# Two plain pairs of feature tiles in the first FFN, rms made before the token sums, squares summed on DVE, unit loads issued six units ahead

## The chip, the cores and the metric

The kernel runs on one core of a Trainium2 chip. Its engines work side by side, each through its own list of instructions, and wait for one another by semaphores: PE (TensorE: matmuls; PEld is its loading of weights), DVE (VectorE), ACT (ScalarE), POOL (GpSimd) and SP (SyncE, which issues DMAs only). The metric is the device time of one launch in microseconds (us), the median over runs; lower is better.

## The reference, cut to what matters

One layer of a streaming encoder on 512 tokens of width 1024, in fp32. The change touches the two FFNs and the sums of squares ahead of them; the mixer between them stays.

```python
def rms_norm(x, w):
    return x * lax.rsqrt(jnp.mean(x * x, axis=-1, keepdims=True) + EPS) * w

def swiglu(h, w_gate, w_up, w_down):
    return (jax.nn.silu(h @ w_gate) * (h @ w_up)) @ w_down

# x (1, 512, 1024); w_gate, w_up (1024, 2816); w_down (2816, 1024)
x = x + 0.5 * swiglu(rms_norm(x, ffn1_norm), ffn1_w_gate, ffn1_w_up, ffn1_w_down)
x = x + hybrid_mixer(x, mix_norm, w_in, ..., w_out)      # SSD and chunked attention
x = x + 0.5 * swiglu(rms_norm(x, ffn2_norm), ffn2_w_gate, ffn2_w_up, ffn2_w_down)
return rms_norm(x, final_norm)
```

## The kernel before, in words

**Layout and precision.** x lies in SBUF as 8 blocks k of 128 model columns (partitions) by 512 tokens. An fp32 product is three matmuls on values rounded to a shorter type: hi x hi, hi x lo, lo x hi (`mm3`, L154 to L156). So every operand is split: ACT casts the high part, DVE subtracts it from the source for the low part. `usplit` does it for an FFN unit's weights of 128x1024 (L284, L286), `wsplit` for other weights (L102, L104), `split_act` for x times the norm's gain (ACT, and DVE at L162).

**An FFN.** The 22 feature tiles of 128 are 11 pairs d. A pair needs gate and up; the columns of x are halved into k 0 to 3 and k 4 to 7, which gives four weight units of 512 KB: A11 and A12 (gate, first and second half), A21 and A22 (up). Pair 0 is done plain: four units, each 8 products of `mm3` at 512 columns. Every later pair is done by a scheme of seven products P1 to P7 in place of eight half-sized ones (as in Strassen's): each of its units has the 24 matmuls at 256 columns (L479), half of the tokens. It wants sums of token halves and sums of weight units. The token sums are made by `XCombos` out of x: `weigh` (x times the gain, L384 and L386, into a buffer xw), `sum1` (L390), `sums23` (L394, L395), `sum4`, and their splits `parts1`, `parts23` (L405) and `parts4`; `parts1` is written over the second half of what `base` made (b1), which the plain units read. The weight sums are made by DMAs that POOL issues and that add onto a tile in SBUF (`more`, L323).

**rms.** The norm's factor is put in at the end, on the finished gate and up. ACT squares x, `add_squares` adds the squares up (L170, on POOL in the two openings), `rstd_begin` sums over partitions on PE (L198) and makes the root by a chain of tiny instructions on DVE (L173 to L191) and two low and high diagonals (L210), `spread` (L217) brings the factor to all partitions with two matmuls, and ACT copies it twice into rstd (L586). `plain_end` then makes h of the plain pair: L459 takes the finished gate out of its PSUM buffer, L464 the up.

**Order.** `program` lists the units: A11 A21 A12 of pair 0, P5 P1 of pair 1, A22, P6 P2 P7, then for every further pair seven units, of which P3 and P4 belong to the pair before, and the down projection's units ("D") in three blocks. `Stream.get` hands out the next unit; before it does, it splits units up to `look` ahead and issues the loads of units ahead of that, each with its own lead in units (the first number of a job's moves). Raw weights lie in four buffers `raw`; the weight sums in others. Between units the generator `early1` or `early2` runs one piece of the work on x and rms. That is the order in which the instructions are written; a scheduler then orders each engine's list by what is ready, so a list can differ from it. PSUM has three buffers mm and five aux. Loads go out on SP's queue, accumulating loads on POOL's.

**Second FFN's opening.** The output projection (`wo`, its products at L1111, the residual add into x at L1112) ends block by block; for each block the loop adds onto x, calls `base` and squares, and the second FFN's first units are split between them.

Of the kernel before, what the change touches and what calls it, by code (L numbers as in the profile page):

```python
# [12 lines left out]
ALU = mybir.AluOpType  # L13

P = 128
# [14 lines left out]
NL = 3  # L30
# [8 lines left out]
def hybrid_block(ctx: ExitStack, tc, xT, par, wgu1, wd1, win, wdt, wv, wo, rbt, wgu2, wd2, out):  # L39
# [67 lines left out]
    class Job:  # L107
# [15 lines left out]
    class Stream:  # L123


        def __init__(self):
            self.jobs, self.done, self.used, self.look = [], 0, 0, 3

        def add(self, dram, n, c):
# [145 lines left out]
    HSLOT = (22, 26, 36, 44)  # L275
# [27 lines left out]
    def ffn_weights(wgu, wd, n_last=0):  # L303
# [9 lines left out]
        def plain(key, src):  # L313
# [11 lines left out]
        for step in program(n_last):  # L325
            if step[0] == "P":
# [3 lines left out]
                if p[0] == "A":  # L330
                    n = ("A11", "A12", "A21", "A22").index(p)
                    j = Job(lambda p=p: usplit(bufs[p]), (5, None, plain(p, A[n])))
                elif p == "P1":
                    j = Job(lambda d=d: usplit(bufs["g", d]), (5, None, plain(("g", d), A[0])))
# [13 lines left out]
                jobs[p, d] = j  # L348
                ws.jobs.append(j)
# [81 lines left out]
    def ffn(xc, early, after, last=None, n_last=0):  # L431
# [13 lines left out]
        def plain(p):  # L445

            if not st:
# [797 lines left out]
```

## Time and profile before

| | |
|---|---|
| median of 3 runs | 1057.44 us (1057.33 to 1059.22) |
| the profiled execution, its span | 1058.14 us, 1056.4 us |
| granted clock of TensorE, mean of the span | 0.99 |
| PE, DVE, ACT, POOL busy | 97%, 72%, 52%, 14% |

The span is from the first to the last instruction of the profiled execution; its own time holds some 1.7 us around it. Times on the trace count from the span's start. A row of the waits says which engine (and which destination) waited for which engine's instruction: us in total, how often, the longest. A row of the timeline is a group of like instructions that follow each other: start, length, engine, line, operation, destination <- sources, shapes, count, and in brackets what the engine waited for ahead of it. A row of the stretches gives the busy time of PE, PEld, DVE, ACT and POOL, then the granted clock (1.00 is 2.4 GHz, 0.50 is 1.2 GHz), the share of the DMA engines, and GB/s.

### The profile page before, as it was taken

Reading aid. Unit: us, or ns where it says so; the run is one execution under the profiler, and the core shown is the slowest. Engines: PE = TensorE matmul, PEld = TensorE weight load, DVE = VectorE, ACT = ScalarE, POOL = GpSimd, SP = SyncE. Lnnn points to the kernel's source line nnn. Section 1 sums busy time; section 2 is a strip of 40 time slices with the busy share of each in tenths; the row PEclk is TensorE's granted clock in tenths of the full one; section 3 lists DMA queues with packets and bytes.
Section 4 is the critical chain, followed back from the end, with each engine's and each line's share of the span. In section 5 each row is a group of like instructions: output and inputs, shape, how many; then the busy total and the mean of one; then the engine's idle time right before and its main releaser. Section 6 shows DMA issues by size and latency. Waiting matters only on the chain. (4 is left out here: it accounts for less than half of the span.)

```text
span 1056.4 us, 16176 instructions
## 1 busy us (share of the span) xinstructions
PE 1026.2 (97%) x6350; PEld 915.2 (87%) x6350; DVE 757.1 (72%) x1224; ACT 547.2 (52%) x869; POOL 150.1 (14%) x163
## 2 busy tenths in 40 slices
PE   8799999999999999999999999899999999999996
PEld 6799989998899787878888788679998899989975
DVE  6987645684377778988867999797784378644754
ACT  6565424562254556656656875555552255522543
POOL 3411100110010003313201111230110011000000
PEclk9899999999999999999999999999999999999998
DMA  9878744883362422121232232926994388643612
GB/s 325 185 181 231 181 139 107 209 216 88 100 138 88 135 62 79 61 81 60 67 112 66 77 100 81 272 62 145 216 238 125 101 200 201 157 120 96 133 52 81
DMA packets 42877, 141.70 MB, mean 134 GB/s; under 512 B 4528, under 2 KB 7344, under 8 KB 42800
## 3 DMA queue, kind: packets, MB, share of 16 engines
q1 hardware_dynamic: 29040, 95.69, 27.2%
q0 software_dynamic: 11520, 41.95, 22.5%
q10 hardware_dynamic: 2240, 3.02, 0.9%
q8 instruction: 50, 0.82, 0.3%
q14 instruction: 27, 0.22, 0.1%
HBM read 138.55 MB, written 2.10 MB: 133 GB/s over the span
## 5 line engine op out<-in xcount | busy, mean ns | idle before, releaser
L479 PE MATMUL mm<-s,xw 128*128 128x256 f32 x1920 | 242.2, 284 | 0.0
L479 PEld LDWEIGHTS mm<-s,xw 128*128 128x128 f32 x1920 | 236.8, 193 | 0.2
L479 PE MATMUL aux<-s,xw 128*128 128x256 f32 x1440 | 185.7, 285 | 6.2 <-ACT xw L284 3.5
L102 ACT CAST whi<-raw 128x512 fp32r<-128x512 f32 (+1 forms) x178 | 106.0, 603 | 159.1 <-PE mm L155 121.6
L479 PEld LDWEIGHTS aux<-s,xw 128*128 128x128 f32 x1440 | 180.0, 194 | 8.0 <-ACT xw L284 3.9
L104 DVE TENSOR_TENSOR wlo<-raw,whi 128x512 fp32r<-128x512 f32 (+1 forms) x178 | 122.4, 692 | 55.6 <-ACT whi L102 55.1
L154 PE MATMUL mm<-s,whi 128*128 128x512 f32 x366 | 143.1, 392 | 4.8 <-DVE x L1112 3.1
L155 PE MATMUL mm<-s,whi 128*128 128x512 f32 x366 | 143.3, 392 | 0.0
L156 PE MATMUL mm<-s,wlo 128*128 128x512 f32 x366 | 143.2, 391 | 0.0
L284 ACT CAST xw<-raw 128x1024 fp32r<-128x1024 f32 x87 | 91.3, 1049 | 98.5 <-PE mm L479 44.1
L286 DVE TENSOR_TENSOR xw<-raw,xw 128x1024 fp32r<-128x1024 f32 x87 | 109.7, 1261 | 43.8 <-ACT xw L284 43.1
L154 PE MATMUL mm<-xw,whi 128*128 128x512 f32 x288 | 118.0, 410 | 0.0
L284 ACT CAST xw<-s 128x1024 fp32r<-128x1024 f32 x60 | 62.8, 1047 | 101.5 <-PE aux L479 61.4
L155 PE MATMUL mm<-xw,whi 128*128 128x512 f32 x288 | 113.0, 392 | 0.0
L156 PE MATMUL mm<-xw,wlo 128*128 128x512 f32 x288 | 112.9, 393 | 0.0
L323 POOL DMA_DIRECT2D s<-wgu x60 | 52.9, 905 | 402.6 <-DVE xw L286 256.9
L286 DVE TENSOR_TENSOR xw<-s,xw 128x1024 fp32r<-128x1024 f32 x60 | 73.2, 1220 | 27.0 <-ACT xw L284 27.0
L154 PEld LDWEIGHTS mm<-s,whi 128*128 128x128 f32 x366 | 69.0, 189 | 20.5 <-ACT s L384 3.5
L514 DVE TENSOR_TENSOR x<-x,mm 128x512 f32<-128x512 f32 x45 | 30.9, 687 | 74.6 <-PE mm L156 74.6
L155 PEld LDWEIGHTS mm<-s,whi 128*128 128x128 f32 x366 | 69.1, 189 | 14.4 <-DVE s L510 0.4
L156 PEld LDWEIGHTS mm<-s,wlo 128*128 128x128 f32 x366 | 69.1, 189 | 14.4
L155 PEld LDWEIGHTS mm<-xw,whi 128*128 128x128 f32 x288 | 54.3, 188 | 11.8 <-issue 1.2
(260 smaller groups left out, 1428.8 us busy)
## 6 DMA issues: line engine op xcount, KB each, us to landing
raw<-wgu SPq DMA_DIRECT2D x67, 512.0 KB, 4.4
s<-wgu POOLq DMA_DIRECT2D x60, 512.0 KB, 5.8
raw<-wd SPq DMA_DIRECT2D x32, 512.0 KB, 5.0
raw<-win SPq DMA_DIRECT2D x28, 512.0 KB, 3.5
s<-wgu SPq DMA_DIRECT2D x20, 512.0 KB, 5.6
raw<-wgu POOLq DMA_DIRECT2D x20, 512.0 KB, 6.4
raw<-wd SPq DMA_DIRECT2D x16, 384.0 KB, 3.3
raw<-wo SPq DMA_DIRECT2D x12, 512.0 KB, 3.6
```

Source lines behind the costliest of these rows:

```text
L102: S.copy(out=hi, in_=src)
L104: V.tensor_tensor(out=lo, in0=src, in1=f(hi), op=ALU.subtract)
L154: T.matmul(ps, lhsT=sh, rhs=mh, start=start, stop=False, skip_group_check=skip)
L155: T.matmul(ps, lhsT=sh, rhs=ml, start=False, stop=False, skip_group_check=skip)
L156: T.matmul(ps, lhsT=sl, rhs=mh, start=False, stop=stop, skip_group_check=skip)
L284: S.copy(out=hi, in_=src)
L286: V.tensor_tensor(out=lo, in0=src, in1=f(hi), op=ALU.subtract)
L323: return lambda: G.dma_start(out=get(), in_=src, accum_op=ALU.add)
L479: T.matmul(ps[:, j * HS:(j + 1) * HS], lhsT=sw[:, j, k], rhs=m, start=(p in ("P1", "P2", "P5") and j == 0 and k == 0 and n == 0), stop=(k ...
L514: V.tensor_tensor(out=x[:, o], in0=x[:, o], in1=ps, op=ALU.add)
```

## The change

The first FFN does two pairs plain, so pairs 0 and 1 take eight plain units in a row and the seven-product scheme begins with pair 2; the second FFN keeps one plain pair, with P1 ahead of P5. The generators are written anew: in the first FFN the squares and rms come first and the token sums behind them, `parts1` only behind A21 of pair 1, since it overwrites what that unit reads. In the second FFN rms comes with the first sums. Squares are added on DVE everywhere. The tiles of h change places (HSLOT). A plain pair 1 takes its PSUM buffers from both kinds. Loads of raw units have a lead of six units instead of five (P2 and P4 five instead of four, P5's first nine instead of ten), and a raw load is issued only when the job that holds the buffer four loads before has been split (`ws.raws`, `holds`). The diff, cut:

```diff
-            self.split, self.moves, self.parts = split, list(moves), None
+            self.split, self.moves, self.parts, self.holds = split, list(moves), None, self
...
             while self.moves and (force or ahead <= self.moves[0][0]):
                 lead, after, fn = self.moves[0]
+                if after == "raw":
+
+                    after = ws.raws[-4] if len(ws.raws) > 3 else None
+                    if not after or after.parts is not None:
+                        ws.raws.append(self.holds)
                 if after and after.parts is None:
                     assert not force
                     return
...
-                moves = [(5, None, lambda: raw.append(load(dram, n, c)))] if a == 0 else []
+                moves = [(5, "raw", lambda: raw.append(load(dram, n, c)))] if a == 0 else []
+            jobs[0].holds = jobs[-1]
...
-    def add_squares(acc, src, first, eng=None):
+    def add_squares(acc, src, first):
         if first:
             S.activation(out=acc, in_=src, func=AF.Square)
         else:
             sq = sb("fh", [P, SEQ], bufs=2)
             S.activation(out=sq, in_=src, func=AF.Square)
-            (eng or V).tensor_tensor(out=acc, in0=acc, in1=sq, op=ALU.add)
+            V.tensor_tensor(out=acc, in0=acc, in1=sq, op=ALU.add)
...
-    HSLOT = (22, 26, 36, 44)
+    HSLOT = (36, 44, 22, 26)
...
-    def program(n_last):
-
-
-        out = [("P", p, d) for p, d in (("A11", 0), ("A21", 0), ("A12", 0), ("P5", 1), ("P1", 1), ("A22", 0), ("P6", 1),
-                                        ("P2", 1), ("P7", 1))]
-        for d in range(2, ND):
+    def program(plain, n_last):
+
+
+        if plain == 1:
+            out = [("A11", 0), ("A21", 0), ("A12", 0), ("P1", 1), ("P5", 1), ("A22", 0), ("P6", 1), ("P2", 1), ("P7", 1)]
+        else:
+            out = [(a, d) for d in range(plain) for a in ("A11", "A21", "A12", "A22")]
+            out += [(p, plain) for p in ("P5", "P1", "P6", "P2", "P7")]
+        out = [("P", p, d) for p, d in out]
+        for d in range(plain + 1, ND):
             out += [("P", p, e) for p, e in (("P5", d), ("P1", d), ("P3", d - 1), ("P4", d - 1), ("P6", d), ("P2", d),
                                              ("P7", d))]
...
-                    j = Job(lambda p=p: usplit(bufs[p]), (5, None, plain(p, A[n])))
+                    j = Job(lambda k=(p, d): usplit(bufs[k]), (6, "raw", whole((p, d), A[n])))
...
                 elif p == "P2":
-                    j = Job(lambda d=d: usplit(bufs["g2", d]), (4, None, plain(("g2", d), A[1])))
+                    j = Job(lambda d=d: usplit(bufs["g2", d]), (5, "raw", whole(("g2", d), A[1])))
                 elif p == "P4":
-                    j = Job(lambda d=d: usplit(bufs["u2", d]), (4, None, plain(("u2", d), A[3])))
+                    j = Job(lambda d=d: usplit(bufs["u2", d]), (5, "raw", whole(("u2", d), A[3])))
                 elif p == "P5":
-                    j = Job(lambda d=d: usplit(view(d)), (10, jobs.get(("P3", d - 4)), first(d)),
+                    j = Job(lambda d=d: usplit(view(d)), (9, jobs.get(("P3", d - 4)), first(d)),
                             (7, None, more(sum_, A[3])))
...
+                if p == "P7":
+                    jobs["P1", d].holds = j
...
-        def plain(p):
-
-            if not st:
-                st["A1"], st["A2"] = [mmps(), mmps()], [aux(), aux()]
+        def plain(p, d):
+
+            if p == "A11":
+                st["A1", d] = [mmps(), aux() if d else mmps()]
+            elif p == "A21":
+                st["A2", d] = [mmps(), mmps()] if d else [aux(), aux()]
             wh, wl = ws.get()
             for k in range(4):
                 for j in range(2):
-                    mm3(st["A" + p[1]][j], wh[:, j, k], wl[:, j, k], *xc.moving(p, k), p[2] == "1" and k == 0,
+                    mm3(st["A" + p[1], d][j], wh[:, j, k], wl[:, j, k], *xc.moving(p, k), p[2] == "1" and k == 0,
                         p[2] == "2" and k == 3)
...
-        def plain_end():
-            th, tl = h_tiles(0)
...
+                done = next(early, None)
+                if done is not None:
+                    plain_end(done)
...
     def rstd_both(rs, dg):
         pb = aux()
@@ -586,37 +603,35 @@
             S.activation(out=r, in_=pb, func=AF.Copy, scale=scale)
             rs.append(r)
 
-    def early(xc, rs, acc, squares):
-
-        for k in range(KD):
-            xc.weigh(x[:, k], k)
-        xc.sum1()
-        ws.look = max(ws.look, 2)
-        yield
-        xc.parts1()
-        squares(range(0, 4))
-        ws.look = 3
-        yield
-        xc.sums23()
-        for k in range(4):
-            xc.parts23(k)
-        squares(range(4, KD))
-        yield
-        dg, _ = rstd_begin(acc, D)
-        yield
-        xc.sum4()
-        yield
-        rstd_both(rs, dg)
-        yield True
-        xc.parts4()
-        yield
-
     def early1(rs):
         for k in range(4, 8):
             xc1.base(x[:, k], k)
         yield
         acc = sb("acc", [P, SEQ])
-        yield from early(xc1, rs, acc, lambda ks: [add_squares(acc, x[:, k], k == 0, G) for k in ks])
+        for k in range(KD):
+            add_squares(acc, x[:, k], k == 0)
+        ws.look = 2
+        yield
+        dg, _ = rstd_begin(acc, D)
+        ws.look = 3
+        yield
+        rstd_both(rs, dg)
+        yield 0
+        for k in range(KD):
+            xc1.weigh(x[:, k], k)
+        yield
+        xc1.sum1()
+        xc1.parts1()
+        yield
+        xc1.sums23()
+        yield
+        yield 1
+        for k in range(4):
+            xc1.parts23(k)
+        xc1.sum4()
+        yield
+        xc1.parts4()
+        yield
         S.copy(out=dw[:, :, 0:16], in_=dtw)
         S.copy(out=dw0[:, :, 0:16], in_=dtw)
...
+    ffn(xc1, 2, early1, after1)
...
@@ -1111,11 +1126,27 @@
             mm3(ps, wh[:, 0, a], wl[:, 0, a], ath[k], atl[k], k == 0, k == 3)
         V.tensor_tensor(out=x[:, o], in0=x[:, o], in1=ps, op=ALU.add)
         xc3.base(x[:, o], o)
-        add_squares(accs[1], x[:, o], o == 0, G)
+        add_squares(accs[1], x[:, o], o == 0)
 
     def early2(rs):
-        yield
-        yield from early(xc3, rs, accs[1], lambda ks: None)
+        for k in range(KD):
+            xc3.weigh(x[:, k], k)
+        yield
+        xc3.sum1()
+        dg, _ = rstd_begin(accs[1], D)
+        yield
+        xc3.parts1()
+        rstd_both(rs, dg)
+        yield
+        xc3.sums23()
+        yield
+        for k in range(4):
+            xc3.parts23(k)
+        yield
+        xc3.sum4()
+        yield 0
+        xc3.parts4()
+        yield
...
+    ffn(xc3, 1, early2, after2, last=last2, n_last=NL)
```

The next rows are the order of instructions on an engine: line, operation, destination <- sources by names with numbers, shape. Lines of the kernel after differ: L286 is L292 there, L191 L197, L162 L168, L170 L176, L217 L223, L386 L398, L394 L406, L1112 L1127. First DVE in the first FFN's opening, where the chain of rms (rq) begins, before:

```order
L286 TENSOR_TENSOR xw_97_420<-raw_162,xw_96_418 128x1024
L191 TENSOR_SCALAR rq_v_386<-aux_381 128x4
L405 TENSOR_TENSOR s_115_537<-s_40_136,s_114_536 128x512
L175 TENSOR_SCALAR rq_t_388<-rq_v_386 128x4
L405 TENSOR_TENSOR s_117_539<-s_40_136,s_116_538 128x512
L177 TENSOR_SCALAR rq_y_390<-rq_t_388 128x4
```

And now:

```order
L176 TENSOR_TENSOR acc_230<-acc_230,fh_250 128x512
L292 TENSOR_TENSOR xw_87_326<-raw_161,xw_86_324 128x1024
L197 TENSOR_SCALAR rq_v_292<-aux_287 128x4
L398 TENSOR_SCALAR s_40_136<-x_62,par_61 128x512
L181 TENSOR_SCALAR rq_t_294<-rq_v_292 128x4
L402 TENSOR_TENSOR s_40_136<-s_40_136 128x4x256
L183 TENSOR_SCALAR rq_y_296<-rq_t_294 128x4
L292 TENSOR_TENSOR xw_89_330<-raw_203,xw_88_328 128x1024
L187 TENSOR_TENSOR rq_q_298<-rq_y_296 128x4
L406 TENSOR_TENSOR s_40_136<-s_40_136 128x4x256
L189 SCALAR_TENSOR_TENSOR rq_r_300<-rq_q_298,rq_v_292 128x4
```

The chain stands behind the last of DVE's own adds of squares, and now has the weighing and sums of x (s_40, 128x1024 each) and a unit's split between its tiny instructions, where it had splits of token sums of 128x512.

Second PE, where it spreads the factor of rms (the operands s_92 or s_82, and acc, against onesr) in the first FFN, before:

```order
L479 MATMUL mm_291<-s_39_135,xw_69_299 128x256
L479 MATMUL mm_291<-s_38_134,xw_70_301 128x256
L217 MATMUL aux_481<-s_92_410,onesr_82 128x512
L479 MATMUL aux_292<-s_24_120,xw_76_351 128x256
L479 MATMUL aux_292<-s_25_121,xw_76_351 128x256
```

And now:

```order
L161 MATMUL mm_384<-s_31_127,xw_88_328 128x512
L162 MATMUL mm_384<-s_30_126,xw_89_330 128x512
L223 MATMUL aux_358<-s_82_316,onesr_82 128x512
L160 MATMUL aux_385<-s_16_112,xw_66_257 128x512
L161 MATMUL aux_385<-s_17_113,xw_66_257 128x512
L223 MATMUL aux_358<-acc_317,onesr_82 128x512
L162 MATMUL aux_385<-s_16_112,xw_67_259 128x512
```

The spread stood between units of the seven-product scheme; it now stands between plain units of pair 1, behind 24 matmuls into the third mm buffer (mm_384) and ahead of the 24 into an aux buffer (aux_385), and its second matmul comes three places later.

Third DVE in the output projection ahead of the second FFN (L1112, then L1127, is the residual add that frees an mm buffer, xw the split of an FFN unit, wlo that of an output weight), before:

```order
L104 TENSOR_TENSOR wlo_6833<-raw_6717,whi_6831 128x512
L1112 TENSOR_TENSOR x_62<-x_62,mm_6835 128x512
L162 SCALAR_TENSOR_TENSOR s_1315_6760<-x_62,par_61,s_1314_6759 128x512
L286 TENSOR_TENSOR xw_1371_6955<-raw_6909,xw_1370_6953 128x1024
L162 SCALAR_TENSOR_TENSOR s_1317_6762<-x_62,par_61,s_1316_6761 128x512
L104 TENSOR_TENSOR wlo_6856<-raw_6808,whi_6854 128x512
L1112 TENSOR_TENSOR x_62<-x_62,mm_6860 128x512
```

And now:

```order
L1127 TENSOR_TENSOR x_62<-x_62,mm_6742 128x512
L292 TENSOR_TENSOR xw_1367_6864<-raw_6792,xw_1366_6862 128x1024
L168 SCALAR_TENSOR_TENSOR s_1310_6667<-x_62,par_61,s_1309_6666 128x512
L176 TENSOR_TENSOR acc_6689<-acc_6689,fh_6733 128x512
L168 SCALAR_TENSOR_TENSOR s_1312_6669<-x_62,par_61,s_1311_6668 128x512
L176 TENSOR_TENSOR acc_6689<-acc_6689,fh_6758 128x512
L104 TENSOR_TENSOR wlo_6763<-raw_6715,whi_6761 128x512
L1127 TENSOR_TENSOR x_62<-x_62,mm_6769 128x512
```

Two adds of squares (L176) have come into DVE's list between two residual adds, and the unit's split stands one scaled split earlier.

## Rows read from the trace of the kernel before

**Rows 1.** The page, part 1: busy us, share of the span, instructions.

```profile
PE 1026.2 (97%) x6350; PEld 915.2 (87%) x6350; DVE 757.1 (72%) x1224; ACT 547.2 (52%) x869; POOL 150.1 (14%) x163
```

**Rows 2.** Waits of TensorE: us in total, times, longest us.

```profile
PE mm L154 <- DVE x L1112: 3.8, 3, 3.1
PE aux L479 <- ACT xw L284: 3.5, 1, 3.5
PE aux L479 <- DVE s L405: 2.7, 3, 1.2
...
PE aux L198 <- POOL acc L170: 1.1, 1, 1.1
...
PE aux L217 <- DVE s L210: 0.9, 1, 0.9
```

**Rows 3.** Stretches: length, busy us by engine, clock, DMA share, GB/s.

```profile
30.00:35.00 5.00, 3.83 (x18) 3.53 (x18) 5.00 (x2) 0.00 (x0) 4.75 (x5) 0.50 0.93 158
595.00:600.00 5.00, 3.49 (x23) 2.83 (x22) 4.95 (x13) 4.42 (x11) 0.00 (x0) 1.00 0.22 84
670.00:685.00 15.00, 13.51 (x59) 10.59 (x57) 10.12 (x11) 7.28 (x13) 5.06 (x4) 1.00 1.02 283
690.00:695.00 5.00, 4.43 (x17) 3.18 (x15) 4.93 (x7) 1.36 (x3) 1.93 (x2) 0.85 0.75 137
```

**Rows 4.** Timeline of TensorE: start us, us, line, tiles, shapes, count.

```profile
12.97 0.39 PE L154 MATMUL aux<-s,xw 128*128 128x512 f32 x1
...
23.65 0.39 PE L156 MATMUL mm<-s,xw 128*128 128x512 f32 x1
...
46.38 4.52 PE L479 MATMUL mm<-s,xw 128*128 128x256 f32 x24
...
55.24 3.04 PE L479 MATMUL mm<-s,xw 128*128 128x256 f32 x24
58.12 3.04 PE L479 MATMUL aux<-s,xw 128*128 128x256 f32 x24
```

**Rows 5.** Timeline of DVE in the opening.

```profile
10.43 0.75 DVE L162 SCALAR_TENSOR_TENSOR s<-x,par,s 128x512 fp32r<-128x512 f32 x1
12.18 1.23 DVE L286 TENSOR_TENSOR xw<-raw,xw 128x1024 fp32r<-128x1024 f32 x1 [1.00 <-ACT xw L284]
13.32 0.88 DVE L386 TENSOR_SCALAR s<-x,par 128x512 f32<-128x512 f32 x2
...
18.42 3.94 DVE L162 SCALAR_TENSOR_TENSOR s<-x,par,s 128x512 fp32r<-128x512 f32 x2
...
23.62 1.21 DVE L394 TENSOR_TENSOR s<-s 128x1024 f32<-128x1024 f32 x1
24.76 1.21 DVE L286 TENSOR_TENSOR xw<-raw,xw 128x1024 fp32r<-128x1024 f32 x1
...
46.45 0.67 DVE L405 TENSOR_TENSOR s<-s,s 128x512 fp32r<-128x512 f32 x1
...
47.12 0.68 DVE L405 TENSOR_TENSOR s<-s,s 128x512 fp32r<-128x512 f32 x1
...
53.68 1.29 DVE L459 TENSOR_TENSOR fa<-mm,rstd 128x512 f32<-128x512 f32 x2 [0.25 <-ACT rstd L586]
```

**Rows 6.** Timeline of POOL in the opening.

```profile
18.64 3.17 POOL L170 TENSOR_TENSOR acc<-acc,fh 128x512 f32<-128x512 f32 x2
...
53.84 0.85 POOL L323 DMA_DIRECT2D raw<-wgu  x1 [3.28 <-DVE xw L286]
```

**Rows 7.** Timeline of all engines at the second FFN's opening.

```profile
678.84 1.05 ACT L284 CAST xw<-raw 128x1024 fp32r<-128x1024 f32 x1 [3.92 <-DMA raw<-wgu]
...
681.22 2.78 DVE L286 TENSOR_TENSOR xw<-raw,xw 128x1024 fp32r<-128x1024 f32 x1
...
681.29 3.83 POOL L170 TENSOR_TENSOR acc<-acc,fh 128x512 f32<-128x512 f32 x2
...
686.19 0.67 DVE L1112 TENSOR_TENSOR x<-x,mm 128x512 f32<-128x512 f32 x1
```

More of the change, by code (lines that the diff above doesn't have):

```diff
@@ L126, in __init__ @@
         def __init__(self):
-            self.jobs, self.done, self.used, self.look = [], 0, 0, 3
+            self.jobs, self.done, self.used, self.look, self.raws = [], 0, 0, 3, []
         def add(self, dram, n, c):
@@ L301, in program, with ffn_weights @@
         return out + [("D", 2, o, c) for o in range(2, KD - n_last) for c in range(2)]
-    def ffn_weights(wgu, wd, n_last=0):
+    def ffn_weights(wgu, wd, plain, n_last=0):
         bufs, jobs = {}, {}
@@ L311, in view, with whole @@
             return bufs[d]
-        def plain(key, src):
+        def whole(key, src):
             def go():
@@ L323, in more @@
             return lambda: G.dma_start(out=get(), in_=src, accum_op=ALU.add)
-        for step in program(n_last):
+        for step in program(plain, n_last):
             if step[0] == "P":
@@ L331, in ffn_weights @@
                     n = ("A11", "A12", "A21", "A22").index(p)
-                    j = Job(lambda p=p: usplit(bufs[p]), (5, None, plain(p, A[n])))
+                    j = Job(lambda k=(p, d): usplit(bufs[k]), (6, "raw", whole((p, d), A[n])))
                 elif p == "P1":
-                    j = Job(lambda d=d: usplit(bufs["g", d]), (5, None, plain(("g", d), A[0])))
+                    j = Job(lambda d=d: usplit(bufs["g", d]), (6, "raw", whole(("g", d), A[0])))
                 elif p == "P2":
-                    j = Job(lambda d=d: usplit(bufs["g2", d]), (4, None, plain(("g2", d), A[1])))
+                    j = Job(lambda d=d: usplit(bufs["g2", d]), (5, "raw", whole(("g2", d), A[1])))
                 elif p == "P4":
-                    j = Job(lambda d=d: usplit(bufs["u2", d]), (4, None, plain(("u2", d), A[3])))
+                    j = Job(lambda d=d: usplit(bufs["u2", d]), (5, "raw", whole(("u2", d), A[3])))
                 elif p == "P5":
-                    j = Job(lambda d=d: usplit(view(d)), (10, jobs.get(("P3", d - 4)), first(d)),
+                    j = Job(lambda d=d: usplit(view(d)), (9, jobs.get(("P3", d - 4)), first(d)),
                             (7, None, more(sum_, A[3])))
@@ L429, in moving, with ffn @@
             return [a[:, h] for a in t[k]]
-    def ffn(xc, early, after, last=None, n_last=0):
+    def ffn(xc, n_plain, early, after, last=None, n_last=0):
         st = {}
@@ L463, in plain_end @@
                 h = sb("fh", [P, SEQ], bufs=2)
-                V.scalar_tensor_tensor(out=h, in0=st["A2"][j], scalar=-1.0, in1=s, op0=ALU.mult, op1=ALU.mult)
+                V.scalar_tensor_tensor(out=h, in0=st["A2", d][j], scalar=-1.0, in1=s, op0=ALU.mult, op1=ALU.mult)
                 S.copy(out=th[:, j], in_=h)
                 V.tensor_tensor(out=tl[:, j], in0=h, in1=f(th[:, j]), op=ALU.subtract)
-            del st["A1"], st["A2"]
+            del st["A1", d], st["A2", d]
         def run(p, d):
@@ L516, in ffn @@
         pss = {}
-        for i, step in enumerate(program(n_last)):
+        for i, step in enumerate(program(n_plain, n_last)):
             if step[0] == "P":
                 if step[1][0] == "A":
-                    plain(step[1])
+                    plain(*step[1:])
                 else:
                     run(*step[1:])
-                if next(early, None):
-                    plain_end()
+                done = next(early, None)
+                if done is not None:
+                    plain_end(done)
                 continue
@@ L549, in after1 @@
         add_squares(accs[0], x[:, o], o == 0)
-    ffn_weights(wgu1, wd1)
+    ffn_weights(wgu1, wd1, 2)
     raw0 = sb("raw", [P, 2, 4, P], bufs=4)
+    ws.raws.append(ws.jobs[0])
     for n in range(2):
@@ L577, in first_unit @@
         return hi, lo
-    ws.jobs[0] = Job(first_unit)
+    ws.jobs[0].split, ws.jobs[0].moves = first_unit, []
     def rstd_both(rs, dg):
@@ L1101, in hybrid_block @@
         pass
-    ffn_weights(wgu2, wd2, NL)
+    ffn_weights(wgu2, wd2, 1, NL)
     xc3 = XCombos(C_F2)
```

6 lines of the change are left out of this document (3 added, 3 removed).

## The prediction

> **What bounds the kernel now.** I read the page's first part first: TensorE is busy 97% of the span [rows 1], so a time is won only where TensorE idles or runs at half clock, or where its work shrinks. Then the table of who waited for whom, TensorE alone [rows 2]: of its few waits, those of lines 479, 198 and 217 (3.5, 2.7, 1.1 and 0.9 us) all lie in the opening of the first FFN, and the longest single one outside it, 3.1 us on the residual add of line 1112, lies in the output projection that opens the second FFN. Then the stretches [rows 3]: in the opening TensorE's granted clock is 0.50 in 30 to 35 us, and 0.85 in 690 to 695 us, after those waits; 0.50 is the level of 1.2 GHz. Last the timeline: from 55.24 us on the half-width units follow each other every 2.88 us without a gap [rows 4]. So the steady part has nothing to give, and the two openings have some 14 and 6 us.
>
> **What the change adds to TensorE.** A plain unit is 24 matmuls of 512 columns; 48 of them start between 12.97 and 23.65 us, (23.65 - 12.97)/47 = 0.227 us each, so 5.45 us a unit. A plain pair has 4 units, 21.8 us; a seven-product pair has 7 units of 2.88, 20.2 us [rows 4]. The second plain pair costs 1.6 us more on a full TensorE. That is inside the walk below.
>
> **First FFN, walked along the new order.** Before, the first two pairs are whole when the seventh unit of pair 1 ends at 58.12 and two more units have run: 58.12 + 2 x 2.88 = 63.9 us [rows 4]. Now:
>
> 1. DVE carries the squares' adds. An add of 128x512 takes a slot of 0.60 us: two products that follow each other took 1.29 together, the second 0.69, and from one split to the next with a tiny instruction between them it is 0.67 (46.45 to 47.12), so 0.07 for the tiny one [rows 5]. Three adds stand ahead of the second unit's low half, and ACT casts that unit some 0.9 us later, behind two more squares. The low half was ready at 13.41 (12.18 + 1.23) [rows 5]; I expect 14.3, and as TensorE has four matmuls of the high half to run first it loses some 0.5 us: the third unit ends at 24.4 where it ended at 23.9.
> 2. The column sums of the squares follow there (0.8 us) and the fourth unit ends at 30.6. The scheduler then has 24 matmuls of pair 1 that need only the third free mm buffer: 36.05 us. Then TensorE stands before the spread of rms.
> 3. DVE gets to the chain of rms at 25.3 us. Ahead of the spread's first operand stand six instructions of 128x1024 (a sum starts at 23.62, the split behind it at 24.76: 1.14 each, 6.85), a scaling (0.88 for two, 0.44) and a small split (0.3), five splits of 128x512 (3.0), some twelve tiny ones at 0.07 to 0.11 (1.0) and the operand itself (0.6) [rows 5]: 12.2 us, so 37.5. TensorE waits 1.4 us.
> 4. Spread, half a unit, A21 of pair 1, half a unit, A22 of pair 1: 0.45 + 2.72 + 5.45 + 2.72 + 5.45 = 16.8 us, and both pairs are whole at 54.2 us. By the same slots the product that frees the first mm buffer is done at about 40, before A21 wants it at 40.7.
>
> 54.2 instead of 63.9 is 9.7 us. The waits of rows 2 go because weight sums, rms and token sums are no longer wanted within the first four units; the T parts may not be written before A21 of pair 1 has read what they overwrite (46 us) and have until 54. I take off 0.4 us for two units that wait for a copy behind a cast on ACT: 9.3 us. DMA covers this: no accumulating load is wanted before 54 us, and the eight unit loads need one slot each per 5.45 us. Of the loads issued six ahead I expect nothing: with four raw buffers a load still waits for its slot, and TensorE waits for none of them in the steady part.
>
> Between FFN1 and the output projection the instructions keep their order on every engine, so I count nothing there.
>
> **Second FFN's opening.** ACT waits 3.92 us for the third unit's weights (landed 678.8); DVE then runs a split of 128x1024 in 2.78 us instead of 1.21 while POOL adds squares (3.83 us for two), and the residual add that frees an mm buffer starts at 686.19 [rows 5 to 7]. TensorE stands 3.1 us, and its clock falls behind it [rows 2, 3]. Now the stretch on DVE between the landed cast (679.9) and that add is a split 1.14, two scaled splits of 0.70, two adds of 0.60 and a weight split of 0.60: 4.3 us, so 684.2. That is 1.9 us earlier and leaves a wait of 1.2 us. A wait of this size left the clock at 1.00 in 595 to 600 us, where TensorE was busy 3.49 of 5 us [rows 3]; so I also count the clock's fall as gone, at most half of its 3.4 us, 1.7. Against that the spread comes earlier in TensorE's order and may wait about 0.6 us for DVE. Sum 3.0 us. Unknown here is the second unit's load: its predecessor's split now stands behind two attention splits on DVE, its slot comes free some 2 us later, and the DMA engines are full from 670 to 685 us (share 1.02) [rows 3]. At best nothing waits for it, and 4.5 us are won; at worst the third unit lands so much later that the opening is as long as before: 0. I take 3.0, nearer to the former, since six later instructions of DVE no longer share.
>
> **Squares off POOL.** Beside POOL's adds a scaled split took 1.97 us (3.94 for two), alone 0.75 [rows 5, 6]: each add on POOL costs DVE 1.2 us, more than the 0.60 of doing it there. An accumulating load issued by POOL does not do that: two products of 128x512 took 1.29 us together across one [rows 5, 6].
>
> The Trainium skill, SBUF — State Buffer, section "Who interferes with whom", says that a DVE instruction with two SBUF inputs contends with a GpSimd instruction that reads SBUF, and that the later one is blocked. The rows above agree. The skill's Perfetto Trace Analysis, section "Optimizing Scalar/DVE Operations", advises handing work to other engines, even GpSimd, where DVE is saturated, and doubts it in the same breath for the shared port; by its first half the change goes the wrong way, which is rival B.
>
> **Sum.** 9.3 + 3.0 = 12.3 us off the profiled execution's own 1058.14 us (span 1056.4 and 1.7 around it): 1045.8. The median of the three runs is 0.7 lower, by which it would be 1045.1; I say 1045.7.
>
> **Rivals.**
> A. The second opening wins nothing: the same saturated transfers end its waits, the clock falls again. For it: ACT's wait for a landing comes ahead of DVE's part [rows 7]. Against it: the one split there lost 1.6 us to POOL's company, and it is on the path. Time 1045.7 + 3.0 = 1048.7. Chance 0.20.
> B. DVE becomes the bound of the first opening: eight adds of 0.60, 4.8 us, all show at the spread, and the wait, now 6 us, lets the clock fall (24 half-width matmuls took 4.52 us in such a stretch instead of 2.88 [rows 4], 1.6 us more). For it: DVE is the engine that ends half of the waits in rows 2. Against: the scaled splits lose 1.2 us of company each, four of them. Time 1045.7 + 4.8 = 1050.5, to 1052 with the clock. Chance 0.12.
> C. Slower. The chain of step 3 runs at the pace of company, because POOL issues the accumulating loads in just these 12 us: 24 instead of 12.2. TensorE stands 13 us before the spread and the clock falls twice (3.3): 12.3 - 12 - 3.3 = -3, 1061 us. It turns slower when the chain loses over 9 us. Against: a product beside such an issue kept its pace [rows 5, 6]. Chance 0.04.
> The look-ahead that does nothing is in the forecast already. A remainder of 0.02 is a mix that cancels out.
>
> **How the numbers follow.** Forecast 0.62, its own range 1043 to 1048.5 (walk of the first opening 0.5 better to 1.5 worse, the second between 4.5 and 1.5 won). With A and most of B the range goes to 1051; below, 1042.2 if no wait is left at all in either opening. This measurement can tell 0.2%, about 2 us, from no change: faster 0.94 (forecast, A, B), within 0.02, slower 0.04.
>
> **What would show it.** Right: no TensorE wait over 2 us before 60 us, one of 1 to 2 us before the spread (line 223), A22 of pair 1 ending near 54 us; no stretch of half clock before 50 us; scaled splits of 0.75 us everywhere; TensorE resuming the projection near 685 us on the shifted scale, the clock at 1.00 behind it. Wrong: a wait at the spread of 4 us or more (B, C), or waits of DMA in front of casts on ACT beyond 680 us on that scale (A); and the forecast as a whole if the steady part shows gaps that were not there.

## The result and the profile after

The kernel after takes 1043.14 us, median of 4 runs (1042.67 to 1043.91), against 1057.38 for the kernel before in the same comparison: a ratio of 0.9863, 95% interval 0.9846 to 0.988, or 14.2 us. The profiled executions stand 15.1 us apart (1058.14 and 1043.04; spans 1056.4 and 1041.3), and the account below is made against these. The median lies at the lower end of the prediction's own range, 1043 to 1048.5.

The page, part 1, of the kernel after (busy us, share of the span, instructions), and its largest waits of TensorE:

```profile
PE 1021.1 (98%) x6278; PEld 907.6 (87%) x6278; DVE 740.2 (71%) x1232; ACT 544.9 (52%) x863; POOL 126.2 (12%) x145
```

```profile
PE aux L1211 <- DVE fa L1208: 1.9, 1, 1.9
PE aux L223 <- DVE s L216: 1.8, 2, 1.2
...
PE mm L160 <- DVE x L1127: 0.8, 1, 0.8
```

Against [rows 2] the waits on a weight sum, on token sums and on POOL's squares are gone; what is left of any size in the openings is the spread of rms (L223, once in each) and one residual add of 0.8 us. Both kernels run the same matmuls in the steady parts, so the same instruction of each tells how far ahead the kernel after is. It is 8.8 us ahead from 73 us to the second opening, 14.0 behind that opening and 15.7 behind the tail, and hardly gains or loses in between. The last two, in residual adds of the down projection, before and then after:

```profile
799.80 0.69 DVE L514 TENSOR_TENSOR x<-x,mm 128x512 f32<-128x512 f32 x1 [1.60 <-PE mm L156]
...
1030.46 0.69 DVE L514 TENSOR_TENSOR x<-x,mm 128x512 f32<-128x512 f32 x1 [2.01 <-PE mm L156]
```

```profile
785.81 0.69 DVE L529 TENSOR_TENSOR x<-x,mm 128x512 f32<-128x512 f32 x1 [1.60 <-PE mm L162]
...
1014.79 0.69 DVE L529 TENSOR_TENSOR x<-x,mm 128x512 f32<-128x512 f32 x1 [2.00 <-PE mm L162]
```

At the very end 0.5 us go back: the last two matmuls took 1.22 us at a granted clock of 0.50, against 0.70 us at 0.96 before. That is no effect of the change: old_loads below, with the same order of instructions as the kernel after, took 0.78.

Timeline of TensorE in the first opening, kernel after:

```profile
13.69 0.40 PE L161 MATMUL aux<-s,xw 128*128 128x512 f32 x1
14.35 0.73 PE L162 MATMUL aux<-s,xw 128*128 128x512 f32 x2 [0.26 <-DVE xw L292]
...
37.68 0.50 PE L223 MATMUL aux<-s,onesr 128*128 128x512 f32 x1 [1.22 <-DVE s L216]
...
54.58 3.04 PE L494 MATMUL aux<-s,xw 128*128 128x256 f32 x24
...
62.04 3.13 PE L494 MATMUL mm<-s,xw 128*128 128x256 f32 x24
```

Both pairs are whole at 54.58 us, where the unit that follows them starts; before, the same amount of work was done at 63.88, two units behind the last start in [rows 4]. DVE there:

```profile
13.08 1.22 DVE L292 TENSOR_TENSOR xw<-raw,xw 128x1024 fp32r<-128x1024 f32 x1
14.21 1.41 DVE L168 SCALAR_TENSOR_TENSOR s<-x,par,s 128x512 fp32r<-128x512 f32 x2
...
25.45 0.16 DVE L197 TENSOR_SCALAR rq_v<-aux 128x4 f32<-128x4 f32 x1 [0.76 <-PE aux L204]
25.53 0.48 DVE L398 TENSOR_SCALAR s<-x,par 128x512 f32<-128x512 f32 x1
25.92 0.16 DVE L181 TENSOR_SCALAR rq_t<-rq_v 128x4 int32<-128x4 int32 x1
25.99 1.22 DVE L402 TENSOR_TENSOR s<-s 128x1024 f32<-128x1024 f32 x1
...
36.94 0.69 DVE L216 TENSOR_TENSOR s<-ident,rq_h 128x512 fp32r<-128x512 f32 x1
```

The reader is to see how the chain of rms (25.45) goes one tiny step at a time between sums of over 1 us, and that the two scaled splits, 3.94 us beside POOL in [rows 5], now take 1.41. The clock, 0.50 at this place in [rows 3], and the second opening's stretches (length, busy us of PE, PEld, DVE, ACT, POOL, clock, DMA share, GB/s):

```profile
30.00:35.00 5.00, 5.00 (x24) 4.14 (x23) 5.00 (x11) 4.12 (x7) 1.05 (x2) 1.00 1.01 331
```

```profile
675.00:680.00 5.00, 4.41 (x19) 3.68 (x20) 5.00 (x9) 4.99 (x9) 0.00 (x0) 1.00 1.05 302
680.00:685.00 5.00, 5.00 (x23) 4.03 (x22) 5.00 (x9) 1.52 (x3) 0.86 (x1) 1.00 0.06 23
```

Up to 680 us the DMA engines are as full as before (1.05 against 1.02 in [rows 3]); TensorE waits less and stays at 2.4 GHz. ACT still waits for the loads of the second and the third unit:

```profile
664.11 1.06 ACT L290 CAST xw<-raw 128x1024 fp32r<-128x1024 f32 x1 [2.84 <-DMA raw<-wgu]
...
669.40 1.06 ACT L290 CAST xw<-raw 128x1024 fp32r<-128x1024 f32 x1 [1.44 <-DMA raw<-wgu]
```

The third unit's cast starts 9.4 us earlier than in [rows 7] (678.84), at a place where the kernel is 9.1 us ahead: the transfer itself came only 0.3 us sooner. The gain lies behind it, on DVE: from the end of this cast to the start of the residual add that frees the buffer it is 4.3 us (670.46 to 674.76), before 6.3 (679.89 to 686.19). In DVE's timeline of the kernel after, splits and adds of squares share one engine and nothing takes longer than it does alone (the residual add for which TensorE waits is the last row; its fellow of before, at 686.19, is in [rows 7]):

```profile
670.49 1.23 DVE L292 TENSOR_TENSOR xw<-raw,xw 128x1024 fp32r<-128x1024 f32 x1 [1.01 <-ACT xw L290]
671.64 0.75 DVE L168 SCALAR_TENSOR_TENSOR s<-x,par,s 128x512 fp32r<-128x512 f32 x1
672.30 0.69 DVE L176 TENSOR_TENSOR acc<-acc,fh 128x512 f32<-128x512 f32 x1
...
674.76 0.69 DVE L1127 TENSOR_TENSOR x<-x,mm 128x512 f32<-128x512 f32 x1
```

The third gain is at a place that the prediction does not speak of. ACT ahead of the last block of the second FFN, kernel before and then after:

```profile
1011.22 0.83 ACT L1139 CAST xw<-raw 128x768 fp32r<-128x768 f32 x1 [3.54 <-DMA raw<-wd]
1011.97 0.62 ACT L499 ACTIVATE fs<-fu 128x512 f32<-128x512 f32 x1
```

```profile
995.62 0.63 ACT L514 ACTIVATE fs<-fu 128x512 f32<-128x512 f32 x1 [3.99 <-DVE fu L512]
996.91 0.84 ACT L1170 CAST xw<-raw 128x768 fp32r<-128x768 f32 x1 [0.66 <-PE mm L494]
```

Before, a cast of a weight for the last output blocks waited 3.54 us for its load, and the silu of the last pair stood behind it; TensorE then lost 0.98 and 0.62 us, by the starts of its matmuls, waiting for h. Now the silu stands ahead of that cast, and TensorE does not wait.

### The profile page after: what moved, and what is told of

It is laid out like the page before. It is cut to its first block, busy times and chain, and to the rows that moved or that the text cites. A ratio compares the mean times of both kernels' runs of the same rounds, so it can differ in the third digit from the quotient of the medians.

```text
span 1041.3 us, 15996 instructions
## 1 busy us (share of the span) xinstructions
PE 1021.1 (98%) x6278; PEld 907.6 (87%) x6278; DVE 740.2 (71%) x1232; ACT 544.9 (52%) x863; POOL 126.2 (12%) x145
## 4 chain that ended last, share of the span: by engine, by line
PE 82%; DVE 12%; ACT 2%; issue 1%; DMA 1%; SPq 0%; POOL 0%; DVEq 0%; ACTq 0%
PE mm L494 21%; PE aux L494 16%; PE mm L160 13%; PE mm L161 13%; PE mm L162 13%; DVE fs L687 2%; DVE wlo L104 1%; DMA raw<-wgu 1%; DVE xw L292 1%; PE aux L1047 1%; PE aux L162 1%; DVE s L417 1%; PE aux L160 1%; PE aux L161 1%; PE aux L1069 1%
## 5 line engine op out<-in xcount | busy, mean ns | idle before, releaser
L494 PE MATMUL mm<-s,xw 128*128 128x256 f32 x1824 | 228.8, 283 | 0.0
L494 PEld LDWEIGHTS mm<-s,xw 128*128 128x128 f32 x1824 | 223.2, 192 | 0.6 <-ACT fa L499 0.2
L494 PE MATMUL aux<-s,xw 128*128 128x256 f32 x1368 | 173.7, 283 | 0.0
L494 PEld LDWEIGHTS aux<-s,xw 128*128 128x128 f32 x1368 | 168.9, 192 | 0.6
L162 PE MATMUL mm<-s,wlo 128*128 128x512 f32 x366 | 142.3, 389 | 0.0
L292 DVE TENSOR_TENSOR xw<-raw,xw 128x1024 fp32r<-128x1024 f32 x87 | 106.4, 1223 | 44.3 <-ACT xw L290 43.5
L290 ACT CAST xw<-s 128x1024 fp32r<-128x1024 f32 x57 | 60.0, 1052 | 102.6 <-PE aux L494 59.6
L162 PE MATMUL mm<-xw,wlo 128*128 128x512 f32 x288 | 112.8, 392 | 0.0
L333 POOL DMA_DIRECT2D s<-wgu x57 | 49.7, 882 | 431.2 <-DVE xw L292 263.3
L292 DVE TENSOR_TENSOR xw<-s,xw 128x1024 fp32r<-128x1024 f32 x57 | 69.7, 1222 | 29.1 <-ACT xw L290 29.1
L160 PEld LDWEIGHTS mm<-s,whi 128*128 128x128 f32 x366 | 68.7, 188 | 15.7 <-ACT xw L290 1.2
L162 PEld LDWEIGHTS mm<-s,wlo 128*128 128x128 f32 x366 | 68.7, 188 | 14.2
L160 PEld LDWEIGHTS mm<-xw,whi 128*128 128x128 f32 x288 | 54.2, 188 | 12.0 <-issue 2.2
```

The costliest lines, as they stand in the source:

```text
L160: T.matmul(ps, lhsT=sh, rhs=mh, start=start, stop=False, skip_group_check=skip)
L162: T.matmul(ps, lhsT=sl, rhs=mh, start=False, stop=stop, skip_group_check=skip)
L290: S.copy(out=hi, in_=src)
L292: V.tensor_tensor(out=lo, in0=src, in1=f(hi), op=ALU.subtract)
L333: return lambda: G.dma_start(out=get(), in_=src, accum_op=ALU.add)
L494: T.matmul(ps[:, j * HS:(j + 1) * HS], lhsT=sw[:, j, k], rhs=m, start=(p in ("P1", "P2", "P5") and j == 0 and k == 0 and n == 0), stop=(k ...
```

## The experiments

Spans are those of the profiled executions (kernel after: 1041.3), ratios go against the kernel before on the same chip. Two executions of unchanged code (before and before_ring up to the second FFN) stood 1.3 us apart in the first opening, so one span carries about that much there.

**Undoing the second plain pair.**

```diff
-    ffn_weights(wgu1, wd1, 2)
+    ffn_weights(wgu1, wd1, 1)
-    ffn(xc1, 2, early1, after1)
+    ffn(xc1, 1, early1, after1)
 # early1 now: weigh, sum1 | parts1, squares | sums23, parts23, squares | rstd_begin | sum4 | rstd_both
```

> The kernel after, but the first FFN with one plain pair and the old order (token sums first, rms behind them); squares stay on DVE, the second FFN stays as it is, and the ring of split buffers is set so that the second FFN meets it in the same phase. Theory (room): eight plain units in a row give DVE and the accumulating loads the time they need, and with four the TensorE waits in the opening come back: 5 to 9 us slower, about 1050, with several waits of over 1 us before 50 us. Rival (company): the first opening was won by taking the squares off POOL; then it is within 2 us of the kernel after, 1042 to 1045, since one plain pair less is also 1.6 us less work.

1054.49 us, ratio 0.9966 (0.9953 to 0.9979), span 1053.0: 11.7 slower than the kernel after, 11.1 of it in the first opening; of 1.5 lost in the second, whose code is unchanged, 0.9 come back elsewhere. Waits of TensorE from 6 to 66 us:

```profile
PE aux L223 <- DVE s L216: 4.1, 1, 4.1
PE mm L494 <- DVE s L417: 1.5, 1, 1.5
PE aux L204 <- DVE acc L176: 1.4, 1, 1.4
```

Room holds, and more than expected: the waits are on DVE, the longest is the spread, and half clock follows it (0.53 from 55 to 60 us). It is not a clean undoing, since P1 stays ahead of P5 and the leads and the places of h stay new: its first opening is even 2.3 us longer than that of the kernel before. So 11.1 us is not the price of the pair alone; before_sqv below has the old order whole.

**Squares back on POOL, in the first opening and in the second.**

```diff
-            add_squares(acc, x[:, k], k == 0)              # sq1_pool
+            add_squares(acc, x[:, k], k == 0, G)
-        add_squares(accs[1], x[:, o], o == 0)              # sq2_pool
+        add_squares(accs[1], x[:, o], o == 0, G)
```

> The kernel after with the first FFN's squares added on POOL again. Theory: each of seven adds on POOL slows a split beside it by 1.2 us where an add on DVE takes 0.60, and they end late, so the chain of rms starts later: TensorE's wait before the spread grows from 1.4 to 2 to 6 us, time 1044 to 1048, 1045.6 expected. Rival: DVE has slack enough in the longer opening, no change, 1043.1.

1047.92 us, ratio 0.9906 (0.9891 to 0.9921), span 1046.0: 4.7 slower, 4.3 of it in the first opening. The wait at the spread is 2.9 us and the clock falls to 0.66 from 40 to 45 us. The theory holds, at the upper end of its range.

> The kernel after with only the squares of the output projection's loop added on POOL again. Theory: the 4.6 us won in the second opening come mostly from here: TensorE's wait for the residual add is back at 2.5 to 3.5 us, its clock falls behind it, time 1046 to 1047. Rival (order): they come from the new order of rms and sums, of P1 and of the loads; then at most 1 us slower, no wait over 1.5 us and no half clock before 700 us.

1049.65 us, ratio 0.9919 (0.9906 to 0.9931), span 1047.3: 6.0 slower, and 6.9 in the second opening alone. DVE in its second opening, beside POOL's adds:

```profile
671.09 2.46 DVE L168 SCALAR_TENSOR_TENSOR s<-x,par,s 128x512 fp32r<-128x512 f32 x2
673.47 1.76 DVE L104 TENSOR_TENSOR wlo<-raw,whi 128x512 fp32r<-128x512 f32 x1
...
677.62 2.30 DVE L292 TENSOR_TENSOR xw<-raw,xw 128x1024 fp32r<-128x1024 f32 x1
679.84 1.77 DVE L168 SCALAR_TENSOR_TENSOR s<-x,par,s 128x512 fp32r<-128x512 f32 x1
```

```profile
PE mm L160 <- DVE x L1127: 4.4, 2, 2.5
```

Two waits on residual adds, 1.9 and 2.5 us, and the clock at 0.67 and 0.70 in the stretches behind them (675 to 680, 685 to 690 us). The theory holds; its price was 2 us too low, because it counted one wait.

**The same one-line edit on the kernel before.**

```diff
-            (eng or V).tensor_tensor(out=acc, in0=acc, in1=sq, op=ALU.add)   # callers drop G
+            V.tensor_tensor(out=acc, in0=acc, in1=sq, op=ALU.add)
```

> The kernel before with the squares of both openings added on DVE, and nothing else. Theory: in the first opening, where DVE has no room with one plain pair, 2 us more are lost (as with one plain pair in the kernel after); in the second opening the wait for the residual add shrinks and the clock stays, 2 to 4 us won: between 1 us slower and 2 us faster in all, and the two openings show it apart. Rival: the second opening's gain needs the new order or the ring's new phase: under 1 us is won there, and the whole is 2 us slower or more.

1053.36 us, ratio 0.9959 (0.9947 to 0.9972), span 1051.6: 4.8 faster than before, 2.3 in the first opening and 2.9 in the second, with 0.5 lost again at the last two matmuls: more than either theory gave it. For the first opening both were wrong: DVE has room for the squares even with one plain pair. Besides the wait at the first matmuls, TensorE's waits there from 6 to 66 us are still five of 0.8 to 2.9 us:

```profile
PE aux L479 <- ACT xw L284: 2.9, 1, 2.9
PE mm L479 <- ACT fu L487: 1.5, 1, 1.5
PE aux L217 <- DVE s L210: 1.4, 1, 1.4
PE aux L198 <- DVE acc L170: 1.3, 1, 1.3
...
PE aux L479 <- DVE xw L286: 0.8, 1, 0.8
```

So about a third of the whole gain is the squares alone, and the second plain pair with all that belongs to it takes the other 6.5 us of the first opening. The pair, the order of rms and sums, the places of h and the PSUM buffers were not undone one by one.

**The loads, and the second FFN's order.**

```diff
-  (6, "raw", whole(...)), P2 and P4 (5, "raw", ...), P5 (9, ...), add (5, "raw", ...)     # old_loads
+  (5, None, whole(...)), P2 and P4 (4, None, ...), P5 (10, ...), add (5, None, ...)
-  ("A12", 0), ("P1", 1), ("P5", 1)                                                        # old_early2
+  ("A12", 0), ("P5", 1), ("P1", 1)    and early2's steps in the order that early had
```

> The kernel after with the old leads (5 units, P2 and P4 4, P5's first 10) and without the rule that a raw load waits for the split of the job four loads before. Theory: the loads win nothing, as the buffers set when a load can start: span within 0.5 us of the kernel after (1041.3), waits of TensorE as there. Rival: part of the second opening's 4.6 us comes from them: 1 to 2.5 us slower, with TensorE's waits between 660 and 700 us.

1043.13 us, ratio 0.9854 (0.9836 to 0.9873), span 1040.7: no difference. The order of instructions on PE, DVE, ACT and POOL is that of the kernel after, and the six units of lead and the new rule win nothing that these runs can tell.

> The kernel after with the second FFN's generator in its old order (token sums first, rms behind the fourth step) and P5 ahead of P1; squares stay on DVE. Theory: the new order costs a wait of 0.8 us at the spread and saves little: between 0.8 us faster and 1 us slower than the kernel after. Rival: P1, which needs no weight sum, ahead of P5 and the early rms carry the second opening's gain: 2 to 4 us slower, with a wait of TensorE of over 1 us on the split of a weight sum or on a token sum after 680 us.

1044.95 us, ratio 0.9871 (0.985 to 0.9893), span 1042.7: 1.4 slower, with 2.3 us lost in the second opening; the interval overlaps that of the kernel after. TensorE waits twice for a residual add (3.7 us together) and not at the spread. By the trace the size is the rival's, 2 to 4, but not its mechanism: no weight sum and no token sum is waited for. That the new order wins is likely, not shown.

**The ring's phase, moved back in the kernel after and on in the kernel before.** The first FFN now sends 71 units through the four split buffers instead of 74, so the second FFN starts at another of them, and the last blocks' casts, which use six of their eight tiles, get theirs at another time.

```diff
     xc3 = XCombos(C_F2)
+    turn[0] += 3        # ring_back, on the kernel after
+    turn[0] += 1        # before_ring, on the kernel before
```

> The kernel after with one added line: ahead of the second FFN the counter of the ring of four split buffers is moved on by three, so that the second FFN meets it in the phase that it had before (the first FFN now takes 71 units through it, not 74). Theory: the 1.5 us won ahead of the last block come from this phase, since by it ACT's casts for the last output blocks, which wait for their loads, stand ahead of or behind the silu of the last pair: TensorE stands some 1.6 us in two waits near 1000 us again, time 1044.6. Rival: they come from the leads and the new rule for raw loads, or from the places of h: 1043.1, and no such waits.

1046.97 us, ratio 0.9899 (0.9885 to 0.9913), span 1044.6: 3.3 slower, some 1.2 of it ahead of the last block, where ACT's rows are those of before again:

```profile
998.92 0.84 ACT L1171 CAST xw<-raw 128x768 fp32r<-128x768 f32 x1 [3.58 <-DMA raw<-wd]
999.66 0.63 ACT L514 ACTIVATE fs<-fu 128x512 f32<-128x512 f32 x1
```

The other 2.1 us are in the second opening (four waits, 3.0 us together), which neither theory expected.

> The kernel before with one added line: the counter of the ring of four split buffers is moved on by one ahead of the second FFN, so that the second FFN meets the ring in the phase that it has in the kernel after. Theory: the phase alone wins some 3 us (1.2 to 1.5 ahead of the last block and about 2 in the second opening, as moving it back cost the kernel after 3.3): ratio to before 0.997. Rival: the second opening is bound by the squares on POOL whatever the phase, and only the tail's 1.2 to 1.5 us are won: ratio 0.9987.

1059.81 us, ratio 1.0011 (1.0001 to 1.002): nothing won. The tail does what the theory says (1.8 us won, no wait of TensorE on h there), but the second opening loses 2.8 us, with two waits on residual adds:

```profile
PE mm L154 <- DVE x L1113: 6.4, 2, 3.4
```

The phase fixes the tail in both kernels; in the opening the new phase helps the kernel after and harms the kernel before, by little more than the 1.5 us that unchanged code there lost in one_plain. Why is not settled: it decides when the first unit's buffers come free, hence when the later units' loads go out, but I did not separate this from the squares.

**A version that should beat both: the chain of rms with nothing between its steps.**

```diff
-        dg, _ = rstd_begin(acc, D)
+        dg, r = rstd_begin(acc, D)
+        late = sb("rq_c", [P, KD])          # chain_64: [P, 2 * KD]; chain_pt: late = pt[:, C_F1:C_F1 + KD]
+        for h in (0, 4):                    # gains = 0 * r + gains; weigh reads late
+            V.scalar_tensor_tensor(out=late[:, h:h + 4], in0=r, scalar=0.0,
+                                   in1=pt[:, C_F1 + h:C_F1 + h + 4], op0=ALU.mult, op1=ALU.add)
```

> The kernel after, in the first FFN with the weighing of x for the token sums tied behind the root of rms (the gains go through two tiny instructions that read it), so that no sum of 128x1024 can stand between the tiny ones of the chain. Theory: TensorE's wait of 1.4 us at the spread and the 0.43 us on the second unit's low half go, and nothing new comes: 1.8 us faster, span 1039.5. Rival: the token sums come too late for the first unit of pair 2 and its fellows (from 54 us on): a new wait there of 1 to 3 us, no gain or a loss.

1047.12 us, ratio 0.989 (0.9873 to 0.9906), span 1044.7: 3.4 slower. Yet at 119 us it was 1.8 us ahead, without a wait at the spread and without one for token sums. From there on it lost steadily, with no waits: its matmuls of 512 columns on split weights (whi, wlo) started 232 ns apart (median), 227 in the kernel after, at a granted clock of 1.00; those of 256 columns kept their 120. Three runs settle what that was.

> The kernel chain_first with its added tile of gains 64 instead of 32 bytes long per partition. In chain_first the first opening was 1.8 us shorter, as expected, but the matmuls of 512 columns on split weights then followed each other every 232 ns instead of 227, at a granted clock of 1.00; every tile allocated behind the added one lay 32 bytes further on, off a multiple of 64. Theory (address): with 64 bytes the pace is 227 ns again and the 1.8 us stay: span 1039.5, time 1041.3. Rival: the pace came from something else in chain_first (the order, the clock): 1044.7 again.

1047.87 us, ratio 0.9902 (0.9888 to 0.9915), span 1046.2, 233 ns: 64 bytes are no better than 32, and the theory of a multiple of 64 falls.

```diff
+        G.memset(sb("rq_c", [P, KD]), 0.0)      # pad_32, on the kernel after: a tile that nobody reads
```

> The kernel after with a dead tile of 32 bytes per partition, set to zero once by POOL and read by nobody, allocated at the same place as chain_first's. Theory (address): the matmuls of 512 columns on split weights follow each other every 232 ns, and with nothing else changed the kernel is about 5.2 us slower than the kernel after: span 1046.5. Rival: nothing changes, 1041.3.

1048.5 us, ratio 0.9916 (0.9902 to 0.9929), span 1046.8, as the theory says. The order of instructions on PE, DVE and ACT is that of the kernel after. The in-projection in TensorE's timeline, kernel after and then pad_32:

```profile
430.08 0.39 PE L160 MATMUL mm<-xw,whi 128*128 128x512 f32 x1
...
431.44 0.39 PE L160 MATMUL mm<-xw,whi 128*128 128x512 f32 x1
```

```profile
430.69 0.40 PE L160 MATMUL mm<-xw,whi 128*128 128x512 f32 x1
...
432.10 0.40 PE L160 MATMUL mm<-xw,whi 128*128 128x512 f32 x1
```

Six matmuls in 1.36 us there, in 1.41 here: 227 and 235 ns each. A dead tile of 32 bytes costs 5.4 us of this kernel.

The down projection of pad_32 narrows down why. For each output it takes 12 matmuls on h of two pairs whose tiles lie behind the added one, as the split weights do, and then 12 on h of two pairs whose tiles lie ahead of it and kept their place:

```profile
122.17 0.39 PE L160 MATMUL mm<-s,whi 128*128 128x512 f32 x1
...
123.53 0.40 PE L160 MATMUL mm<-s,whi 128*128 128x512 f32 x1
...
124.93 0.40 PE L160 MATMUL mm<-s,whi 128*128 128x512 f32 x1
```

The six up to 123.53, on h that moved together with the weights, take 1.36 us, 227 ns each; the six behind, on h that did not move, take 1.40, 233 each. So it goes in every output of the first FFN's first two blocks: the first six matmuls, which follow slow ones, have a median of 230 ns, the next six 227, the last twelve 232 to 235; in chain_first it is the same, in chain_64 231, 227 and 233.

> The kernel chain_first, with the gains written back in place into the table of parameters instead of a new tile, so that every tile lies where it lies in the kernel after; the order on PE and DVE is that of chain_first. Theory (placement): the pace of the matmuls of 512 columns on split weights is 227 ns again and the 1.8 us of the first opening stay: span 1039.5, time 1041.3, faster than both kernels. Rival: the slow pace belongs to the order of chain_first: 1044.7.

1041.61 us, ratio 0.9845 (0.9832 to 0.9859), span 1039.8: 1.5 faster than the kernel after by the spans (1.8 expected) and the fastest of all; the intervals of the two ratios overlap, so this rests on the traces. The pace is 227 ns. DVE, chain and first operand:

```profile
25.50 0.16 DVE L197 TENSOR_SCALAR rq_v<-aux 128x4 f32<-128x4 f32 x1 [1.37 <-PE aux L204]
25.69 0.17 DVE L181 TENSOR_SCALAR rq_t<-rq_v 128x4 int32<-128x4 int32 x1
...
29.19 0.68 DVE L216 TENSOR_TENSOR s<-ident,rq_h 128x512 fp32r<-128x512 f32 x1
```

3.7 us from the first tiny step to the operand, against 11.5 in the kernel after, and TensorE does not wait for it.

## Why the prediction was right, and where it was off

**First opening: right, term by term.** Predicted 9.7 us by the walk, less 0.4 for two units that wait for a copy: 9.3. Measured 9.3 where the pairs are whole (54.58 for 54.2), and 8.8 behind those two units. By the times they came as said: the units at 62.04 and 66.72 start 0.05 us after copies out of PSUM on ACT end (61.99, 66.67), each copy behind a cast, and lose 0.25 us each. The low half of the second unit was ready at 14.3, as said; it cost 0.43 for 0.5; the spread's operand came at 37.6 for 37.5, the wait at 1.2 to 1.4 for 1.4. What carried it was counting DVE's slots in the new order, no more. That the total came within 0.5 us is partly luck, since the first opening of unchanged code varied by 1.3.

**Second opening: right in mechanism, too small.** Predicted 3.0 us, measured 5.2, above the 4.5 named as the best case. The long stall shrank by 2.3 us (3.25 to 0.94 by the starts of the matmuls; 1.9 in the sum), the half clock went (1.6 for 1.7) and the spread cost 0.8 (0.6, for which the prediction gave no row). The step that failed is the choice of terms: [rows 2] says three waits on the residual add, 3.8 us, and the sum priced only the one of 3.1. By the starts of the matmuls the other two are worth 1.3 us with the slow restart behind them, a wait on a token sum at 713.53, which the prediction had put into the first opening with the rest of its row, 0.6, and one on ACT's split of the attention at 670.71 some 0.35: together 2.2, the size of the miss. In sq2_pool a second wait on a residual add comes back with the first. The feared load of the second unit came later, some 4 us at the shifted place; ACT waited 2.84 us for it, TensorE did not. Rival A fell: the transfers were as saturated and the third unit landed only 0.3 us sooner, and the gain was there. DVE's part behind the landed cast, 4.3 us in the sum, took 4.3.

**Tail: a term that was not there, 1.7 us.** "TensorE waits for none of them in the steady part" is true of the loads, and old_loads shows no worth of their lead. But the prediction counted nothing at the end. The order of ACT had moved at the tail, by a counter that the number of plain pairs shifts, and the trace of before had the price: a cast 3.54 us behind its load with a silu behind it. ring_back and before_ring both move this wait with one line.

**Rivals.** B, DVE as the bound of the first opening, does not decide here: the adds fit in, and before_sqv wins with them even in the old order. Its mechanism exists, though: in one_plain DVE makes the spread wait 4.1 us and the clock falls. C did not come: POOL issued accumulating loads at 30.21 and 34.81 us, within the chain, and a sum of 128x1024 and a split of 128x512 beside them took 1.22 and 0.69 us, as alone. The squares alone won 4.8 us in the kernel before; in the second opening the rows show why, a slowed split stands ahead of a residual add, and for the first it is argued. Here the rows of sq2_pool (2.30 for a split of 1.23, 1.77 for 0.75) agree with what the Trainium skill, SBUF — State Buffer, section "Who interferes with whom", says of two-input DVE instructions beside a GpSimd instruction that reads SBUF.

**The sum.** 8.8 + 5.2 + 1.7 = 15.7 us at the last residual adds, less 0.5 at the last two matmuls, against 15.1 between the profiled executions; predicted 9.3 + 3.0 = 12.3. So the time fell into the range with one opening priced 2.2 us too low, one 0.5 too high and a tail that was not counted. What stays open is how the second opening's 5.2 divide: undone one at a time, by the traces there, the squares cost 6.9, the order 2.3, the phase 2.1 and the loads 0.6, together 11.9, so each undoing brings back the same waits in part. Only the squares stand clear: one_plain, with the edits of the kernel after in that opening, was 1.5 us worse there too.

## What to carry to other kernels

Price every wait of a row, not its longest, and follow a rotating buffer's phase through the whole program: a change in how many tiles the first stage takes can reorder an engine's list in the last. Walk the waiting engine's new list slot by slot; that gave the waits of the first opening, and its total to within what one execution can tell. And before believing a new order to be slow, look whether the pace of unchanged instructions has changed.

## What the runs showed of the hardware that was not expected

A tile of 32 or 64 bytes per partition, added ahead of others, made most of TensorE's 512-column matmuls on split weights start every 232 to 235 ns instead of 227, at a granted clock of 1.00, 5.4 us in all (pad_32), while 256-column ones stayed at 120. Without the tile the same order on PE ran at 227 (chain_pt). All tiles behind it, the split weights and half of h among them, lay 32 or 64 bytes further on. It is not the place of the weights alone: their matmuls with the half of h that had moved as far kept 227 (pad_32, 122.17 to 123.53 us), those with the half that had not moved took 232 to 235, and so did the in-projection, whose other operand had not moved. In these runs the pace fell where the two operands of a matmul had moved against each other by 32 or 64 bytes; other distances, and which property of the two addresses it is, were not tried.
